# Wider transfers of queries, outputs and cached keys in attention, top-k in two mixed groups, gates split at 10, and an order planned with longer issue times

## The chip, the cores and the metric

The kernel runs on one core of one Trainium2 chip, as one launch. The metric is the time of a run on the device in microseconds (us); lower is better. A core has TensorE (matmuls; PE in the profile, PEld for its weight loads), VectorE (DVE), ScalarE (ACT), GpSimd (POOL) and SyncE (SP), which here issues nearly all transfers between memory (HBM) and the chip's buffers. The engines run beside each other, each through its own list of instructions, strictly in order, and wait for each other by semaphores.

## The reference

One layer of a hybrid encoder, for 1024 new positions of one stream (the prompt) and 32 positions of another (the sample), which has 512 positions of cached keys and values. The weights are shared, all data is float32.

```python
h = rmsnorm(x, g_mix)                          # 1024 + 32 rows of 1024
q_a, k_a, v_a, q_i, k_i, w_i, q_b, k_b, v_b, gate_a, gate_b = split(h @ w_in)
# mixer A: 8 heads of 64, q and k normed and rotated
score = sum over 8 index heads of relu(q_i . k_i) * w_i      # the indexer
keep the 256 best keys per row (136 in the sample), of blocks of 64 that are not later
o_a = softmax(q_a . k_a / 8 over the kept keys) @ v_a
# mixer B: 8 heads of 64, stick-breaking attention, strictly causal
o_b = (sigmoid(z) * product over the later keys of (1 - sigmoid(z))) @ v_b
m = sigmoid(gate_a) * (o_a @ w_branch_a) + sigmoid(gate_b) * (o_b @ w_branch_b)
h = x + m @ w_out
y = h + relu(rmsnorm(h) @ w_up)**2 @ w_down     # 1024 -> 4096 -> 1024
```

The outputs are y of both streams and the new keys and values.

## The kernel before

**Matmuls in three passes.** TensorE multiplies in a shortened float32 (`F32R`). To keep the precision every operand is split into a high part and the rest, and a product is made of three matmuls, high x high, high x rest and rest x high (`three`, line 438). A weight comes in units of 128 x 512: `unit` (line 406) loads one into `wst` (3 buffers), ACT casts it to `wh`, POOL subtracts to `wl` (`split`, line 401; 5 buffers each). `column_block` (line 445) runs the matmuls of one output block over its column chunks.

**Stages** (`Layer.run`, line 464). First come normalisation and the index projections, the projections of mixer B (`project_b`), the index scores, top-k, the projections of mixer A (`project_a`) and gates 0 to 5. Each projection stores queries, keys and values, already split, in device memory (`dq`, `dk`, `dv`). Then comes attention in two rounds. The early round takes the first 512 positions: for mixer B, then for A, for each of 8 heads `attend(h, is_a, (0, 2))` (line 1072), and behind heads 2 and 5 `attend_new` (line 1132), which does the sample for four heads at once. Columns of gates 6 to 15 stand beside it as filler. Then `branch` (line 1225) multiplies the outputs with the branch weights, `out` with `w_out`, and `ffn_group` (line 1274) runs up and down projections of the first 512 positions. The late round of attention, for positions 512 to 1023, is a generator, `late`, that is advanced beside this work, EARLY steps before the branch of mixer A and one step for every PACE units in the FFN. At last the second group, the other 512 positions and the sample, goes through `load_o`, `branch`, `out` and the FFN.

**Order by a planner.** The program is not issued as written. `Plan.record` (line 260) notes every instruction with its dependencies and a cost from `cost` (line 203); `Plan.run` (line 332) simulates the five engines with these costs, and always issues, on the engine that is free first, the ready instruction of the best rank, then the earliest in the program. Ranks are FAST, PREP (loads and splits of weights), MAIN, FILL (the matmuls of `column_block`) and SLOW (top-k). So filler matmuls fall where the planner sees a gap. The order on each engine is fixed by this; on the chip an instruction that is late by the plan's times holds everything behind it on its engine. An issue on SP costs 450 ns in the plan, whatever its shape. `Plan.close` (line 134) first issues everything that touches the buffers to be closed; what is recorded later comes behind it on every engine.

**Attention.** For a head, `attend` loads keys `kk` and values `v` (rings of 2), and for each of two tiles of 256 queries two halves of `q` (high and rest, 64 rows each; ring of 3, [128, 2, 256]). Score matmuls go into banks `s`; `softmax_weights` or `stick_weights` makes the weights; TensorE transposes them into banks `t`, `split_pt` splits them, and the product with `v` goes into `po`. `finish` (line 1053) adds the two halves of `po` into an output `o` [64, 256] and stores it in `do`. `attend_new` loads, per head, the cached keys twice (into both halves of the rows, buffer `k32` in the ring of `q`), the new keys, the cached values and the new values, one transfer each.

**Top-k** (`top_k_begin`, line 778, and `top_k`, line 846). The threshold of every row is found bit by bit, 31 bits. In each bit a candidate (`cand`) is tried: count the scores on one side of it, compare the count with the wanted one (`hit`, in a bank called `small`) and keep the candidate where it hits. Tiles of 128 rows have 128 (t + 1) scores a row; tile 8 is the sample with 32 rows of 544. Three groups run beside each other: `v` with tiles 2, 3 and 4, counted on DVE by a comparison with a sum, and `a` (6, 7) and `b` (5, 8), counted on ACT by Sign with a sum. `top_k` then makes the masks; for groups counted on ACT it first finds the lowest kept score (`low`).

**Gates.** `gate(e)` (line 1184) makes 128 gate columns of all 1056 positions in three chunks (`parts`: 512, 272, 272), with two weight units. For e from 6 to 15 the first chunk is done in one call and the other two in a second call, which loads and splits the two units again; SPLIT = 14 says how many of the second calls stand ahead of the branch of mixer B.

Of the kernel before, what the change touches and what calls it, by code (L numbers as in the profile page):

```python
# [27 lines left out]
H = 8  # L28
# [15 lines left out]
SPLIT = 14  # L44
EARLY, PACE = 16, 4
# [43 lines left out]
class Plan:  # L89
# [113 lines left out]
    def cost(self, eng, op, out, ins, scalar, kw):  # L203
# [45 lines left out]
        return 450.0, 450.0  # L249
# [140 lines left out]
class Layer:  # L390
# [73 lines left out]
    def run(self):  # L464
# [94 lines left out]
        self.pr = g1.pool  # L559
        for is_a in (False, True):  # L560
# [16 lines left out]
        late = (None for is_a in (False, True) for h in range(H) for _ in self.attend(h, is_a, (4, 6)))  # L577
# [14 lines left out]
        for j in (1, 0):  # L592
            self.load_o(g2, j)
            self.branch(g2, j)
# [183 lines left out]
    def top_k_begin(self):  # L778
# [12 lines left out]
        class Group:  # L791
# [3 lines left out]
            def __init__(g, name, tiles, act, place):  # L795
# [6 lines left out]
                g.zero = nc.tile(tp, [128, n], F32, f"zero{name}")  # L802
                nc.vector.memset(g.thr, 0)
                nc.vector.memset(g.allb, -1)
                nc.vector.memset(g.zero, 0.0)
                for j, t in enumerate(tiles):
                    m, L, k = size(t)
                    nc.vector.memset(g.want[:, j:j + 1], float(L + 1 - 2 * k if act else k))

            def count(g, at, op, act):  # L810
                cnt = nc.tile(tp, [128, g.n], F32, "cnt", tag="cnt" + g.name, bufs=2)
                for j, t in enumerate(g.tiles):
                    m, L, _ = size(t)
                    if m < 128:
                        nc.vector.memset(cnt[:, j:j + 1], 0.0)
                    junk = nc.tile(tp, [128, 1024], BF16, "junk", tag="junk" + g.name, bufs=1)
                    if act:
# [9 lines left out]
            def step(g, at, hit_op, new):  # L827
                cnt = g.count(at, ALU.is_ge, g.act)
# [3 lines left out]
            def bit(g, b):  # L832
                cand = nc.tile(tp, [128, g.n], I32, "cand", tag="cand" + g.name, bufs=2)
                nc.vector.tensor_scalar(cand, g.thr, 1 << b, None, op0=ALU.bitwise_xor)
                g.step(cand.bitcast(F32), ALU.is_le if g.act else ALU.is_ge, cand)
# [3 lines left out]
        for gs in (self.groups,):  # L839
            for g in gs:  # L840
                g.step(g.zero, ALU.is_gt if g.act else ALU.is_lt, g.allb)
            for b in range(30, -1, -1):
                for g in gs:
                    g.bit(b)

    def top_k(self):

        nc, tp, tx, size = self.nc, self.top, self.top, self.size
        for g in self.groups:
# [3 lines left out]
            if g.act:  # L853
                low = nc.tile(tp, [128, g.n], F32, "low" + g.name)
                for j, t in enumerate(g.tiles):
                    m, L, k = size(t)
                    pen = nc.tile(tx, [128, 1024], F32, "pen", tag="pre", bufs=1)
# [6 lines left out]
            above = g.count(tf, ALU.is_gt, False)  # L864
# [188 lines left out]
    def finish(self, po, dst, n=256):  # L1053

        nc, at = self.nc, self.at
        tmp = nc.tile(at, [64, 256], F32, "ov", bufs=1)
        o = nc.tile(at, [64, 256], F32, "o", bufs=2)
        nc.scalar.copy(tmp, po[64:128])
        nc.vector.tensor_add(o, po[0:64], tmp)
        if n < 256:  # L1060
            s = o.rearrange("e (j i t) -> e j i t", i=2, t=DEC)
            o = nc.tile(at, [64, 256], F32, "on", tag="o", bufs=2)
            nc.vector.tensor_add(o[:, :n].rearrange("e (j t) -> e j t", t=DEC), s[:, :, 0], s[:, :, 1])
        with nc.rank(FAST):
            nc.sync.dma_start(dst, o[:, :n])
# [6 lines left out]
    def attend(self, h, is_a, tiles):  # L1072
# [30 lines left out]

        for t0 in tiles[::-1]:
            yield
            c = 128 * t0
            q = nc.tile(at, [128, 2, 256], F32R, "q", bufs=3)
            for s in range(2):
                nc.sync.dma_start(
                    q.bitcast(F32)[HD * s:HD * s + HD], self.dq[g].rearrange("s e t -> e s t")[:, :, c:c + 256])  # L1110
# [19 lines left out]
            self.finish(po, self.do[g, :, c:c + 256])  # L1130

    def attend_new(self, u, is_a):
# [7 lines left out]
        for i in range(2):  # L1140
            src = self.dq[g0:g0 + 4, i, :, new].rearrange("j e t -> e j t")
            for s in range(2):
                nc.sync.dma_start(qz[64 * s:64 * s + 64, i], src)
        for j in range(4):
            k32 = nc.tile(at, [128, PAST], F32, "k32", tag="q", bufs=3)
            for i in range(2):
                nc.sync.dma_start(k32[HD * i:HD * i + HD], a["ck" + sfx][4 * u + j])
            k = nc.tile(at, [128, SEQ], F32R, "kc", tag="k", bufs=2)[:, :LS]
            nc.sync.dma_start(k.bitcast(F32)[:, :DEC], self.dk[g0 + j].rearrange("s e t -> (s e) t")[:, new])
            nc.scalar.copy(k[:, DEC:], k32)  # L1150
            nc.gpsimd.tensor_sub(k[HD:, DEC:], k32[HD:], k.bitcast(F32)[HD:, DEC:])
            for i in range(2):
                q, first, last = self.qz[:, i, 128 * j:128 * j + 128], j + i == 0, j + i == 4
                nc.tensor.matmul(ps0, q, k[:, DEC:], start=first, stop=last)
                nc.tensor.matmul(ps1[:, :DEC], q, k[:, :DEC], start=first, stop=is_a and last)
# [14 lines left out]
        for j in range(4):  # L1170
            vcs = nc.tile(at, [128, 8, 128], F32R, "vcs", tag="v", bufs=2)[:, 0:4]
            vc = nc.tile(at, [128, 4, HD], F32, "vc", tag="o", bufs=2)
            nc.sync.dma_start(vc, a["cv" + sfx][4 * u + j])
            self.split(vcs[:, :, 0:HD], vcs[:, :, HD:], vc)
# [232 lines left out]
```

## Time and profile before

| | |
|---|---|
| time, 3 runs | 1838.2 us median, 1836.76 to 1841.13 |
| the profiled execution's own time | 1837.8 us |
| its span, first to last instruction | 1836.0 us |
| PE busy | 1792.9 us, 11622 matmuls |
| POOL, DVE, ACT busy | 1017.0, 1054.0, 900.0 us |
| loads of queries (`q<-dq`) | 128 of 128 KB |
| stores of outputs (`do<-o`) | 64 of 64 KB |
| gate weight units (`wst<-w_g`) | 52 of 256 KB |

In the profile a row of busy time by stage gives from and to in us, the length, then busy time of PE, PEld, DVE, ACT and POOL (with the number of instructions), then the granted clock of TensorE as a share of full speed, the busy share of the DMA engines and GB/s. Rows of instructions are named out<-in by the program's buffers; all carry line 381, the planner's issuing line, so one goes by buffers. A wait reads: who waited <- for whom: us in total, times, longest. The chain is the list of work and waits that ended last, followed back from the end. SPq is SP's queue of issues.

### The profile page before, as it was taken

To read this page: it belongs to the slowest core of one execution; us is meant where nothing else is said; L and a number is where in the kernel's file an instruction comes from. 1 tells how busy PE (TensorE), PEld (TensorE's weight loads), DVE (VectorE), ACT (ScalarE), POOL (GpSimd) and SP (SyncE) were. 2 spreads that over 40 slices of the span, in tenths; PEclk is the share of its full clock that TensorE was granted. 3 is DMA by queue.
4 is the path that set the end of the run, shared out by engine and by line. 5 is a ranking of instruction groups with operands and counts; after the bars stand their busy time and mean duration, and the time that the engine had idled before them with its cause. 6 is when DMAs were issued, how large, how long until landed. Compare 5 with 4: busy or idle time off the path is not lost.

```text
span 1836.0 us, 33063 instructions
## 1 busy us (share of the span) xinstructions
PE 1792.9 (98%) x11622; PEld 1649.0 (90%) x11622; DVE 1054.0 (57%) x2323; ACT 900.0 (49%) x1854; POOL 1017.0 (55%) x897
## 2 busy tenths in 40 slices
PE   8999999999999999999999999999999999999999
PEld 7899999999978889878888888888799999999999
DVE  7569998688244565678875555533326633333333
ACT  7356778952145676867755444442225422222221
POOL 4722232335256755698885545565558655555553
PEclk9999999999998999999999999999999999999999
DMA  7134443445566777664343343343365333233323
GB/s 256 55 88 130 130 135 103 130 133 149 167 191 179 220 196 221 194 180 148 99 132 110 114 134 117 107 132 96 92 193 160 101 91 93 87 87 93 87 87 95
DMA packets 170101, 243.85 MB, mean 133 GB/s; under 512 B 29904, under 2 KB 80432, under 8 KB 169936
## 3 DMA queue, kind: packets, MB, share of 16 engines
q1 hardware_dynamic: 169504, 241.41, 44.2%
q8 instruction: 92, 1.51, 0.3%
q14 instruction: 73, 0.60, 0.1%
q10 hardware_dynamic: 432, 0.34, 0.1%
HBM read 189.39 MB, written 52.17 MB: 132 GB/s over the span
## 4 chain that ended last, share of the span: by engine, by line
PE 83%; DVE 7%; DMA 3%; issue 2%; POOL 2%; SPq 1%; ACT 1%; ACTq 0%; DVEq 0%; POOLq 0%
PE pj L381 63%; PE s L381 12%; PE t L381 4%; PE o L381 4%; DVE junk L381 2%; POOL pb L381 1%; SPq L381 1%; DMA q<-dq 1%; DVE small L381 1%; DVE xl L381 1%; DVE pre L381 1%; DMA k<-dk 0%; POOL wl L381 0%; POOL p L381 0%; DMA xt<-x 0%
## 5 line engine op out<-in xcount | busy, mean ns | idle before, releaser
L381 POOL TENSOR_TENSOR wl<-wst,wh 128x512 fp32r<-128x512 f32 x424 | 571.5, 1351 | 482.7 <-ACT wh L381 441.4
L381 PE MATMUL pj<-xh,wh 128*128 128x272 f32 (+2 forms) x2048 | 691.4, 338 | 2.1 <-ACT wh L381 0.8
L381 PE MATMUL pj<-xl,wh 128*128 128x272 f32 (+2 forms) x2048 | 692.2, 338 | 0.1
L381 PE MATMUL pj<-xh,wl 128*128 128x272 f32 (+2 forms) x2048 | 689.9, 338 | 1.0 <-POOL wl L381 0.9
L381 ACT CAST wh<-wst 128x512 fp32r<-128x512 f32 x424 | 262.1, 620 | 485.0 <-PE pj L381 392.2
L381 PEld LDWEIGHTS pj<-xh,wh 128*128 128x128 f32 x2048 | 386.9, 189 | 35.3 <-ACT wh L381 1.5
L381 PEld LDWEIGHTS pj<-xh,wl 128*128 128x128 f32 x2048 | 386.8, 189 | 31.1 <-POOL wl L381 1.5
L381 PEld LDWEIGHTS pj<-xl,wh 128*128 128x128 f32 x2048 | 386.7, 189 | 30.8 <-DVE xl L381 0.3
L381 DVE TENSOR_TENSOR y<-pj,y 128x272 f32<-128x272 f32 (+1 forms) x192 | 100.4, 524 | 196.5 <-PE pj L381 196.0
L381 PE MATMUL pj<-gh,wl 128*128 128x272 f32 x640 | 184.4, 289 | 0.0
L381 PE MATMUL pj<-gl,wh 128*128 128x272 f32 x640 | 184.2, 289 | 0.2 <-POOL gl L381 0.2
L381 PE MATMUL pj<-gh,wh 128*128 128x272 f32 x640 | 182.5, 288 | 0.0
L381 DVE TENSOR_TENSOR xl<-ru,xh 128x272 fp32r<-128x272 f32 (+1 forms) x96 | 107.3, 1119 | 95.4 <-ACT xh L381 95.2
L381 DVE TENSOR_TENSOR tt<-t,tt 128x512 fp32r<-128x512 f32 (+2 forms) x168 | 101.1, 622 | 56.4 <-ACT tt L381 54.9
L381 ACT ACTIVATE junk<-score,cand 128x768 bf16<-128x768 f32 (+3 forms) x124 | 119.2, 961 | 23.2 <-DVE cand L381 22.6
L381 DVE TENSOR_TENSOR_SCAN rem<-rem 128x896 f32<-128x896 f32 (+6 forms) x66 | 112.6, 1727 | 25.5 <-ACT rem L381 25.2
L381 ACT CAST tt<-t 128x512 fp32r<-128x512 f32 (+2 forms) x168 | 85.7, 539 | 75.1 <-PE t L381 54.9
L381 PEld LDWEIGHTS pj<-gl,wh 128*128 128x128 f32 x640 | 120.5, 188 | 0.7 <-POOL gl L381 0.6
L381 PEld LDWEIGHTS pj<-gh,wl 128*128 128x128 f32 x640 | 120.3, 188 | 0.0
L381 PEld LDWEIGHTS pj<-gh,wh 128*128 128x128 f32 x640 | 119.8, 188 | 0.3
L381 PE MATMUL s<-k,q 128*128 128x512 f32 (+3 forms) x384 | 102.6, 365 | 10.1 <-DMA q<-dq 8.4
L381 POOL TENSOR_TENSOR p<-p,rem 128x895 f32<-128x895 f32 (+6 forms) x66 | 102.6, 1566 | 14.3 <-DVE rem L381 11.3
(211 smaller groups left out, 2880.8 us busy)
## 6 DMA issues: line engine op xcount, KB each, us to landing
wst<-w_up SPq DMA_DIRECT2D x128, 256.0 KB, 2.7
wst<-w_down SPq DMA_DIRECT2D x128, 256.0 KB, 2.6
q<-dq SPq DMA_DIRECT2D x128, 128.0 KB, 3.1
wst<-w_g SPq DMA_DIRECT2D x52, 256.0 KB, 3.4
k<-dk SPq DMA_DIRECT2D x48, 256.0 KB, 3.2
v<-dv SPq DMA_DIRECT2D x48, 256.0 KB, 3.7
dv<-vs SPq DMA_DIRECT2D x32, 256.0 KB, 2.3
wst<-w_out SPq DMA_DIRECT2D x32, 256.0 KB, 2.8
```

Source lines behind the costliest of these rows:

```text
L381: fn(*args, **kw)
```

## The change

- Queries: `attend` loads the 512 columns of a head's two tiles at once, two transfers instead of four, into a ring of 2 buffers [128, 2, 512]. The first late head uses the place of `qz`.
- Outputs: both tiles of a head go into one `o` [64, 512] and one store; `halves` takes the place of `finish`.
- The sample: `k32` holds the cached keys of two heads in 64 rows, one transfer for a pair instead of four; the new keys of four heads come in one transfer (`kn`), the new values too (`vn`, now in the ring of the keys), cached values in pairs.
- Top-k: two groups, `a` with tiles 2, 3, 4 and 7 and `b` with 5, 6 and 8; tile 7 of `a` and tiles 5 and 6 of `b` are counted on ACT, the others on DVE. DVE counts "less than" now, so that both counts compare alike.
- Gates 6 to 9 do all chunks in one call; 10 to 15 keep the second call, which stands behind the branch of mixer B (SPLIT 14 to 10).
- Late attention: one step is advanced behind the last head but one of the early round (AHEAD), EARLY goes from 16 to 14.
- The plan: an issue on SP costs 470 ns, and 620 ns for up to 64 rows.
- Second group: both `load_o` stand ahead of the branches, with 4 buffers of their own. FFN: the row factors go into `acc` in place of a tile `rb2` of their own, and two down projections (KEEP) of the last quarter but one move behind the last up projection.

```diff
-SPLIT = 14
-EARLY, PACE = 16, 4
+SPLIT = 10
+AHEAD = 1
+KEEP = (6, 7)
+TOPK = (("a", [2, 3, 4, 7], (7,), 0), ("b", [5, 6, 8], (5, 6), 16))
+EARLY, PACE = 14, 4
...
-        return 450.0, 450.0
+        d = 470.0 if out.shape[0] > 64 else 620.0
+        return d, d
...
+                for _ in range(AHEAD if is_a and h == H - 2 else 0):
+                    next(late)
...
         for e in range(6, 16):
-            self.gate(e, "pb", 3, self.parts[:1])
-        for e in range(6, SPLIT):
-            self.gate(e, "pb", 3, self.parts[1:])
+            self.gate(e, "pb", 3, self.parts if e < SPLIT else self.parts[:1])
...
         for j in (1, 0):
-            self.load_o(g2, j)
+            self.load_o(g2, j, "o32", 4)
+        for j in (1, 0):
             self.branch(g2, j)
...
-            def count(g, at, op, act):
-                cnt = nc.tile(tp, [128, g.n], F32, "cnt", tag="cnt" + g.name, bufs=2)
+            def count(g, at, op, act=()):
+                g.cnts = g.cnts[::-1]
+                cnt = g.cnts[0]
...
-                    if act:
+                    if t in act:
                         nc.scalar.activation(
...
-        self.groups = [Group("v", [2, 3, 4], False, 0), Group("a", [6, 7], True, 16), Group("b", [5, 8], True, 32)]
+        self.groups = [Group(*x) for x in TOPK]
...
+    def halves(self, po, o):
+
+        nc = self.nc
+        nc.scalar.copy(o, po[64:128])
+        nc.vector.tensor_add(o, po[0:64], o)
...
+        c = 128 * tiles[0]
+        if late and g == H:
+            qq = nc.tile(at, [128, 2, 512], F32R, "q", tag="qz")
+        else:
+            qq = nc.tile(at, [128, 2, 512], F32R, "q", bufs=2)
+        for s in range(2):
+            nc.sync.dma_start(
+                qq.bitcast(F32)[HD * s:HD * s + HD], self.dq[g].rearrange("s e t -> e s t")[:, :, c:c + 512])
+        o = nc.tile(at, [64, 512], F32, "o", bufs=2)
         for t0 in tiles[::-1]:
             yield
-            c = 128 * t0
-            q = nc.tile(at, [128, 2, 256], F32R, "q", bufs=3)
-            for s in range(2):
-                nc.sync.dma_start(
-                    q.bitcast(F32)[HD * s:HD * s + HD], self.dq[g].rearrange("s e t -> e s t")[:, :, c:c + 256])
...
+        kn = nc.tile(at, [128, 4, DEC], F32R, "kn", bufs=1)
+        nc.sync.dma_start(kn.bitcast(F32), self.dk[g0:g0 + 4, :, :, new].rearrange("j s e t -> (s e) j t"))
         for j in range(4):
-            k32 = nc.tile(at, [128, PAST], F32, "k32", tag="q", bufs=3)
-            for i in range(2):
-                nc.sync.dma_start(k32[HD * i:HD * i + HD], a["ck" + sfx][4 * u + j])
...
+            if j % 2 == 0:
+                k32 = nc.tile(at, [64, 2, PAST], F32, "k32", tag="q", bufs=2)
+                nc.sync.dma_start(k32, a["ck" + sfx][4 * u + j:4 * u + j + 2].rearrange("j e t -> e j t"))
...
+        vn = nc.tile(at, [128, SEQ], F32R, "vn", tag="k", bufs=2)[:DEC, :512].rearrange("t (j e) -> t j e", j=4)
+        nc.sync.dma_start(vn.bitcast(F32), self.dv[g0:g0 + 4, :DEC, NEW].rearrange("j t e -> t j e"))
...
-        rb2 = nc.tile(g.pool, [128, g.w], F32, f"rb2{i}")
+        rb2 = g.acc
...
+            if q == nq - 1:
+                for e in KEEP:
+                    go_down(e, q - 1)
             for e in range(KB):
-                go_down(e, q)
+                if q != nq - 2 or e not in KEEP:
+                    go_down(e, q)
                 beside(1)
```

More of the change, by code (lines that the diff above doesn't have):

```diff
@@ L559, in run @@
         self.pr = g1.pool
+        late = (None for is_a in (False, True) for h in range(H) for _ in self.attend(h, is_a, (4, 6)))
         for is_a in (False, True):
@@ L802, in __init__ @@
                 g.zero = nc.tile(tp, [128, n], F32, f"zero{name}")
+                g.cnts = [nc.tile(tp, [128, n], F32, f"cnt{name}{i}") for i in range(2)]
+                for c in g.cnts:
+                    nc.vector.memset(c, 0.0)
                 nc.vector.memset(g.thr, 0)
@@ L827, in step @@
             def step(g, at, hit_op, new):
-                cnt = g.count(at, ALU.is_ge, g.act)
+                cnt = g.count(at, ALU.is_lt, g.act)
                 nc.vector.tensor_tensor(g.hit, cnt, g.want, op=hit_op)
@@ L834, in bit @@
                 nc.vector.tensor_scalar(cand, g.thr, 1 << b, None, op0=ALU.bitwise_xor)
-                g.step(cand.bitcast(F32), ALU.is_le if g.act else ALU.is_ge, cand)
-        self.groups = [Group("v", [2, 3, 4], False, 0), Group("a", [6, 7], True, 16), Group("b", [5, 8], True, 32)]
+                g.step(cand.bitcast(F32), ALU.is_le, cand)
+        self.groups = [Group(*x) for x in TOPK]
         self.size = size
[L839 to L844, printed above, removed]
+        for g in self.groups:
+            g.step(g.zero, ALU.is_gt, g.allb)
+        for b in range(30, -1, -1):
+            for g in self.groups:
+                g.bit(b)
     def top_k(self):
@@ L863, in top_k @@
                 tf = low
-            above = g.count(tf, ALU.is_gt, False)
+            above = g.count(tf, ALU.is_gt)
             need = nc.tile(tp, [128, g.n], F32, "need" + g.name)
@@ L1129, in attend @@
                             start=j + i == 0, stop=j + i == t0 + 2)
-            self.finish(po, self.do[g, :, c:c + 256])
+            self.halves(po, o[:, c:c + 256])
+        with nc.rank(FAST):
+            nc.sync.dma_start(self.do[g, :, 128 * tiles[0]:128 * tiles[0] + 512], o)
     def attend_new(self, u, is_a):
@@ L1180, in attend_new @@
                                  start=k == 0, stop=False)
-            nc.tensor.matmul(out, vn[:DEC], now[:DEC, :, 32 * j:32 * j + 32], start=False, stop=True)
-        self.finish(po, self.do[g0:g0 + 4, :, new].rearrange("g e t -> e g t"), 128)
+            nc.tensor.matmul(out, vn[:, j], now[:DEC, :, 32 * j:32 * j + 32], start=False, stop=True)
+        o = nc.tile(at, [64, 512], F32, "o", bufs=2)
+        self.halves(po, o[:, :256])
+        s = o[:, :256].rearrange("e (j i t) -> e j i t", i=2, t=DEC)
+        on = o[:, 256:384].rearrange("e (j t) -> e j t", t=DEC)
+        nc.vector.tensor_add(on, s[:, :, 0], s[:, :, 1])
+        with nc.rank(FAST):
+            nc.sync.dma_start(self.do[g0:g0 + 4, :, new].rearrange("g e t -> e g t"), on)
     def gate(self, e, tag="gz", bufs=2, parts=None):
@@ L1289, in done @@
                 r = g.tmp("ru", "pb", 3)
[L1290 removed]
+                nc.vector.scalar_tensor_tensor(r, ps, 0.0, rb2[c], op0=ALU.max, op1=ALU.mult)
                 nc.gpsimd.tensor_mul(r, r, r)
```

51 lines of the change are left out of this document (19 added, 32 removed).

## The prediction

> **What bounds the kernel now.** I read the page first, then busy time by stage, then who TensorE waited for in the worst stage, then the DMA queue's own instructions there.
>
> ```profile
> span 1836.0 us, 33063 instructions
> ...
> PE 1792.9 (98%) x11622; PEld 1649.0 (90%) x11622; DVE 1054.0 (57%) x2323; ACT 900.0 (49%) x1854; POOL 1017.0 (55%) x897
> ```
>
> TensorE is the bound. The profiled execution took 1837.8 us: the span of 1836.0 and 1.8 around it; the median of the runs, 1838.2, lies 0.4 above it. The change leaves TensorE's matmuls as they are, so it can only win back what is not work: 1836.0 - 1792.9 = 43.1 us of idle time, and time at a lower clock. The stages, with busy time of PE, PEld, DVE, ACT and POOL, then the granted clock:
>
> ```profile
> 0.00:200.00 200.00, 188.29 (x1196) 175.70 (x1197) 150.19 (x388) 114.28 (x261) 87.33 (x109) 0.99 0.43 129
> 200.00:300.00 100.00, 94.95 (x595) 93.41 (x595) 88.70 (x360) 77.46 (x165) 30.96 (x30) 0.98 0.46 139
> 300.00:460.00 160.00, 154.64 (x1187) 149.74 (x1186) 131.19 (x357) 95.06 (x216) 69.50 (x71) 1.00 0.43 129
> 460.00:520.00 60.00, 60.00 (x365) 53.83 (x365) 14.40 (x33) 9.92 (x20) 12.85 (x11) 1.00 0.49 148
> 520.00:760.00 240.00, 227.61 (x1426) 203.50 (x1425) 128.98 (x299) 157.00 (x340) 160.51 (x155) 0.97 0.71 208
> 760.00:900.00 140.00, 135.63 (x767) 115.56 (x767) 111.36 (x111) 100.31 (x206) 117.67 (x66) 0.99 0.53 158
> 900.00:1420.00 520.00, 519.18 (x2817) 445.03 (x2816) 265.42 (x494) 230.46 (x431) 315.70 (x250) 1.00 0.41 124
> 573.00:580.00 7.00, 5.05 (x28) 3.87 (x27) 6.51 (x8) 4.17 (x11) 5.28 (x6) 0.97 0.64 178
> 580.00:590.00 10.00, 10.00 (x37) 8.83 (x36) 2.23 (x3) 3.76 (x9) 3.09 (x4) 0.51 0.53 161
> 685.00:689.00 4.00, 4.00 (x21) 4.00 (x20) 1.95 (x13) 1.32 (x3) 2.12 (x3) 0.57 0.84 257
> ```
>
> TensorE's idle time is length minus PE: 11.7 us in the first 200 (mostly the start, which the change does not reach), 5.1 in 200 to 300 and 5.4 in 300 to 460 (top-k, on a full DVE), none in 460 to 520 (gates alone), 12.4 in 520 to 760 (the early attention), 4.4 in 760 to 900, 0.8 in 900 to 1420. The last three rows show a second price: behind an idle stretch of 573 to 580 (1.95 us) the clock is about half for 10 us.
>
> What ends the idle time of 520 to 760 are two kinds of load, 9.8 us in all:
>
> ```profile
> PE s L381 <- DMA q<-dq: 8.4, 6, 2.9
> PE s L381 <- DMA kc<-dk: 1.4, 2, 0.8
> ```
>
> The longest, 2.9 us, is at 681. SP's own instructions just before it, and the chain there:
>
> ```profile
> 678.84 0.55 SPq L381 DMA_DIRECT2D dg<-gz  x1
> 679.45 1.24 SPq L381 DMA_DIRECT2D qz<-dq  x2
> 680.79 1.22 SPq L381 DMA_DIRECT2D q<-dq  x2
> ```
>
> ```profile
> 681.40 2.74 DMA q<-dq
> ```
>
> Each issue starts within 0.2 us of the end of the one before: SP is doing nothing but issuing, and the query load stands last in that line. TensorE waits not for bandwidth but for the queue's turn. The planner books 450 ns for every issue (`cost`, line 203), and here each takes 0.55 to 0.62; so its order is one that SP can't keep.
>
> **Part A, the wider transfers.** Prices of an issue on SP (min/median/max ns, then first and last start):
>
> ```profile
> L381 SPq DMA_DIRECT2D q<-dq x68: 573/586/681, 521.4 to 742.9; - x68
> ...
> L381 SPq DMA_DIRECT2D do<-o x64: 451/482/1604, 541.5 to 1210.0; - x64
> ...
> L381 SPq DMA_DIRECT2D k<-ckb x16: 471/510/596, 535.1 to 601.7; - x16
> ...
> L381 SPq DMA_DIRECT2D kc<-dk x16: 326/456/1237, 536.3 to 709.3; - x16
> ```
>
> In the early attention 16 heads load queries four times each (two tiles, two halves); now twice: 32 fewer, 32 x 0.586 = 18.8 us of SP. Outputs, one per head instead of two: 16 x 0.482 = 7.7. The sample's cached keys were loaded twice per head, 32 in all (half of them the row's `ckb`); now once per pair of heads, 8: 24 x 0.51 = 12.2. Its new keys go from 16 issues to 4, 12 x 0.456 = 5.5, and its new values too, which I price at the least of the keys' row, 12 x 0.326 = 3.9. Together 48 us, a fifth of the stage's 240, are taken off a queue that is overloaded in stretches. I expect the gapless lines to break up, the more so as the new order books 620 ns for transfers of up to 64 rows. One wait is new in kind: a wide query load that finds its slot taken holds SP, and behind it stand the weight loads of the filler; the plan orders by that slot too, so I price it at nothing here and in the second rival at its bound. ACT's and POOL's work on the keys keeps its length: as many columns on fewer rows.
>
> The gain: the 9.8 us of waits; and the clock behind them, (1 - 0.51) x 10 = 4.9 at 580 and (1 - 0.57) x 4 = 1.7 at 685: 16.4. I take 15, for a wide load lands later for the first of its two tiles. Bounds: 0 (next waits take its place), and 12.4 + 0.03 x 240 = 19.6, all idle time and all slow clock of the stage.
>
> Is the clock to be counted? The row at 580 says yes, behind a stretch of 7 us with 1.95 us idle in pieces. The Trainium skill (TensorE: Matmul & The Clock Gate, section "Why this matters for your kernels") asks for no idle gap of over about 3 us, since a whole window of idleness brings the half clock back; by it the stretch at 580 has another cause, and the gain would be 11.5 instead of 16.4. The trace disagrees with it here, since no gap in 573 to 580 can be over 1.95 us.
>
> **Part B, the gates split at 10, one late step fewer.** For gates 10 to 13 the last 544 columns move from before `branch(g1, 1)` to behind it, and stay TensorE filler; for 6 to 9 all columns are now done in one pass, so 8 weight units are neither loaded nor split a second time. A unit costs POOL:
>
> ```profile
> L381 POOL TENSOR_TENSOR wl<-wst,wh 128x512 fp32r<-128x512 f32 x424 | 571.5, 1351 | 482.7 <-ACT wh L381 441.4
> ```
>
> 8 x 1.351 = 10.8 us of POOL go, and as many casts on ACT and loads. POOL is the fullest helper of 760 to 900 (117.67 of 140). There late attention starts 15 steps in instead of 16 (1 + 14), and the moved gates bring TensorE work with little POOL work. The idle 4.4 us and 0.01 x 140 = 1.4 of clock are the bound; I take half, 3. Below nothing it could go only if the moved gates came late; the branch before them needs the same outputs as ever.
>
> **Part C, top-k in two mixed groups.**
>
> ```profile
> L381 ACT ACTIVATE junk<-score,cand x124: 727/983/1162, 186.5 to 384.2; 128x768 bf16<-128x768 f32 x31, 32x544 bf16<-32x544 f32 x31, 128x896 bf16<-128x896 f32 x31, 128x1024 bf16<-128x1024 f32 x31
> L381 ACT ACTIVATION_READ_ACCUMULATOR junk<-score,cand x124: 185/186/201, 187.3 to 384.9; 128x1 f32 x93, 32x1 f32 x31
> L381 DVE TENSOR_SCALAR_CACHE_REDUCE junk<-score,cand x93: 602/745/881, 143.3 to 285.2; 128x384 bf16<-128x384 f32 x31, 128x512 bf16<-128x512 f32 x31, 128x640 bf16<-128x640 f32 x31
> L381 DVE DVE_READ_ACCUMULATOR junk<-score,cand x93: 72/82/86, 143.9 to 286.0; 128x1 f32 x93
> ...
> L381 ACT ACTIVATE junk<-score,zeroa x2: 1028/1086/1145, 196.3 to 197.8; 128x896 bf16<-128x896 f32 x1, 128x1024 bf16<-128x1024 f32 x1
> ```
>
> ```profile
> L381 DVE TENSOR_TENSOR small<-cnt,small x96: 143/165/167, 142.2 to 386.6; 128x2 int32<-128x2 f32 x64, 128x3 int32<-128x3 f32 x32
> L381 DVE TENSOR_SCALAR cand<-small x93: 128/159/163, 142.6 to 380.9; 128x2 int32<-128x2 int32 x62, 128x3 int32<-128x3 int32 x31
> L381 DVE COPY_PREDICATED small<-small,cand x93: 146/168/170, 150.7 to 389.4; 128x2 int32<-128x2 int32 x62, 128x3 int32<-128x3 int32 x31
> ```
>
> ```profile
> L381 POOL TENSOR_SCALAR mask<-pre x7: 636/832/1045, 303.0 to 445.6; 128x384 bf16<-128x384 f32 x1, 128x512 bf16<-128x512 f32 x1, 128x640 bf16<-128x640 f32 x1, 128x896 bf16<-128x896 f32 x1
> ```
>
> DVE now spends per bit 3 x (0.745 + 0.082) + 3 x (0.165 + 0.159 + 0.168) = 3.96 us. The change drops one group's small operations (-0.49) and adds the sample's count of 544 columns, about 0.78 between the 512 and 640 columns of the row, plus 0.08: 4.33, or 31 x 0.37 = 11 us more. ACT loses its shortest count: 31 x (0.727 + 0.186) = 28 us less. But the DVE group of tiles 2, 3 and 4 ran alone from 143, a bit in (285.2 - 143.3)/31 = 4.6 us; tied to tile 7 it starts when tile 7 can be counted, which was at 196 (`zeroa`). So 53/4.6 = 11.5 bits of about 3 us of DVE work, at most 34 us, move back, and 11 come on top, 45 in all, into stretches where DVE has 11.3 (200 to 300), 28.8 (300 to 460) and 45.6 us (460 to 520) free. It fits, and the end moves back. A group's `hit` now waits on DVE for ACT's count as well, with the projections' evacuations queued behind it; the two old ACT groups had that wait too. The chain ends at 445.6 in the trace and must end before TensorE's last filler:
>
> ```profile
> 513.93 1.78 DMA dg<-gz
> ```
>
> That leaves 68 us of cover. I expect the chain to end at 470 to 500, hidden, and to cost TensorE 1 us net where DVE is fuller. Bounds: -12 (idle 5.1 + 5.4 and 0.02 x 100 of clock all gone) to +28 (third rival).
>
> **Part D, the rest.** `load_o` ahead of both branches, KEEP and `acc` in place of `rb2` touch 900 to the end, where at most 0.8 us is idle up to 1420: 0.5 gained.
>
> Sum: -15 - 3 + 1 - 0.5 = -17.5; 1837.8 - 17.5 = 1820.3, **1820 us**.
>
> **The rivals.** *More.* Idle time and slow clock of 200 to 1420 all go: 19.6 + 5.8 + 12.5 + 0.8 = 38.7, so 1799. For it: everything is planned anew with truer times. Against it: 300 to 460 has idle time without SP's doing.
>
> *The stall changes its name.* The new values of the sample (`vn`) now sit in the two-slot ring of the keys, so the second head behind each of the 4 sample parts can load keys only after that part's last matmul. With a landing like the 2.74 us above and one issue, 3.4 us, and 1.7 of clock once: 4 x 3.4 + 1.7 = 15.3, which eats part A: 1820.3 + 15.3 = 1836, no change. The same comes out if the queries wait for their ring (two wide slots for three narrow ones) and not for SP: then the change does not do what it says. Against both: SP's gapless line at 681, and eight tiles in flight against six.
>
> *Top-k outlasts the filler (slower).* One place: the closing of the top-k buffers, behind which every attention instruction stands in the plan. The DVE group of before took 4.6 us a bit where it needed about 3. If the two mixed groups, on a DVE that the projections of 300 to 460 fill to 82%, run at half of DVE, 8.7 us a bit, the bits last to 196 + 31 x 8.7 = 466. The masks then take 389.4 to 445.6 as now, 56, and those of the early group, now done in between (303.0 - 285.2), some 18 more: 540. TensorE is dry from 514: 26 us and 1.7 of clock make 1820.3 + 27.7 = 1848. From an end at about 531 on it eats the whole gain.
>
> **How the numbers follow.** A measurement of this kernel can tell about 0.2%, 3.7 us, from no change. The forecast (by itself 1806, with A and B at their upper bounds and C at half of -12, to 1833, with half of A, no B and C at 3) has 0.62, *more* 0.10, the renamed stall 0.12, the long top-k 0.16. Faster 0.72, same 0.12, slower 0.16. The range, 1802 to 1844, takes in the forecast, the renamed stall and part of the two outer cases.
>
> **What would show it.** Right: waits of TensorE for `q` and `kc` in the early attention under 3 us, clock there 0.99 or more, half the query issues at twice the size, the last `mask<-pre` before 514, PE idle under 32 us in all. Wrong: waits of the same stage for `k<-dk` or for helpers in their place; an idle stretch between the last gate and the first score matmul; DVE groups of top-k that run past 460.

## The result and the profile after

| | before | after |
|---|---|---|
| median | 1837.48 us (6 runs, 1836.24 to 1841.13) | 1818.92 us (6 runs, 1816.52 to 1823.79) |
| the profiled execution's own time | 1837.8 us | 1819.17 us |

After takes 0.99 of the time of before, with a 95% interval of 0.9884 to 0.9916: 1.0% faster, some 18 us. The page of after, with the span, the engines' busy time and the row of query loads (KB each, median us from issue to landing):

```profile
span 1817.4 us, 32617 instructions
...
PE 1782.6 (98%) x11622; PEld 1645.4 (91%) x11622; DVE 1059.0 (58%) x2260; ACT 868.0 (48%) x1776; POOL 1013.3 (56%) x889
...
q<-dq SPq DMA_DIRECT2D x64, 256.0 KB, 5.5
```

TensorE runs the same 11622 matmuls. Its idle time is 1817.4 - 1782.6 = 34.8 us instead of 43.1, and its busy time is 10.3 us less for the same matmuls, part of it time at a lower clock. Busy time by stage of after, in the columns of the prediction's rows:

```profile
0.00:200.00 200.00, 187.39 (x1189) 174.77 (x1190) 136.65 (x318) 111.07 (x251) 87.94 (x109) 0.99 0.42 127
200.00:300.00 100.00, 98.96 (x643) 97.99 (x641) 94.49 (x337) 87.46 (x172) 30.85 (x30) 1.00 0.51 156
300.00:460.00 160.00, 155.95 (x1183) 150.94 (x1184) 151.12 (x396) 70.39 (x158) 74.95 (x73) 1.00 0.43 128
...
520.00:760.00 240.00, 229.62 (x1468) 207.04 (x1468) 139.34 (x312) 152.27 (x345) 155.94 (x151) 0.99 0.72 197
760.00:900.00 140.00, 137.62 (x754) 117.07 (x753) 116.22 (x111) 98.59 (x200) 131.12 (x70) 0.99 0.50 143
```

Length minus the first figure is idle time; I count the clock as busy time x (1 - clock), to which the two digits leave about 1 us of play. From 200 to 460 the idle time went from 10.4 to 5.1 us and the clock of 200 to 300 from 0.98 to 1.00: about 7 us won where the prediction had 1 us lost. From 520 to 760 idle time went from 12.4 to 10.4 and the clock from 0.97 to 0.99: 2.0 + 4.5 = 6.5 us, not the 15 of part A. From 760 to 900 it is 2.0 us. The first 200 us lost 0.9. These stages make 15 of the 18.6 us between the two profiled executions. Behind 900, where part D works, TensorE is idle for 4.4 us instead of 4.2, so no gain of it shows; the rest of the 18.6 is busy time that the two digits of the clock can't place.

Who TensorE waited for in 520 to 760, in after:

```profile
PE s L385 <- DMA k<-dk: 4.6, 2, 2.9
PE o L385 <- DVE tt L385: 3.1, 1, 3.1
PE s L385 <- DMA q<-dq: 1.3, 1, 1.3
```

The waits for queries fell from 8.4 to 1.3, as forecast, but waits for keys and for a helper stand in their place, which the prediction had named as a sign of being wrong. The longest wait for a load is at 665. Below are SP's instructions, then TensorE's, then the chain there, then busy time around it (clock, DMA share and GB/s at the end of a row):

```profile
659.50 0.55 SPq L385 DMA_DIRECT2D wst<-w_g  x1
660.14 0.48 SPq L385 DMA_DIRECT2D do<-o  x1
661.05 0.70 SPq L385 DMA_DIRECT2D k<-dk  x1
```

```profile
665.47 0.40 PE L385 MATMUL pj<-xl,wh 128*128 128x512 f32 x1
668.76 0.66 PE L385 MATMUL s<-k,q 128*128 128x384 f32 x1 [2.89 <-DMA k<-dk]
```

```profile
661.05 7.57 DMA k<-dk
```

```profile
660.00:664.00 4.00, 4.00 (x19) 3.25 (x18) 1.15 (x5) 1.52 (x4) 1.88 (x2) 1.00 1.09 265
664.00:668.00 4.00, 1.87 (x9) 1.16 (x7) 0.69 (x1) 2.54 (x4) 0.14 (x2) 1.00 1.04 265
668.00:672.00 4.00, 3.24 (x12) 2.94 (x13) 0.87 (x3) 1.74 (x5) 2.59 (x3) 0.59 0.74 179
```

The keys leave at 661.05 and land only 7.57 us later, while all 16 DMA engines are full (share over 1). Before the wait TensorE has its filler; the next instruction in its fixed order is the score matmul, so it stands for 2.89 us, and behind that the clock is 0.59 for 4 us. At the wait of before at 681 SP issued without a gap; here it is idle from 660.62 (660.14 + 0.48) to 661.05, just ahead of this issue.

Top-k of after, rows of counts and of masks (min/median/max ns, first to last start):

```profile
L385 DVE TENSOR_SCALAR_CACHE_REDUCE junk<-score,cand x124: 601/752/882, 193.2 to 355.2; 128x384 bf16<-128x384 f32 x31, 128x512 bf16<-128x512 f32 x31, 128x640 bf16<-128x640 f32 x31, 32x544 bf16<-32x544 f32 x31
```

```profile
L385 POOL TENSOR_SCALAR mask<-pre x7: 513/833/1258, 374.3 to 438.6; 128x384 bf16<-128x384 f32 x1, 128x512 bf16<-128x512 f32 x1, 128x640 bf16<-128x640 f32 x1, 128x1024 bf16<-128x1024 f32 x1
```

The bits run from 193.2 to 355.2 on DVE, (355.2 - 193.2)/31 = 5.2 us each (the last count on ACT starts at 356.9), and the last mask starts at 438.6, earlier than the 445.6 of before and not at 470 to 500.

### The profile page after: what moved, and what is told of

It reads as the page before. It is cut to its first block, busy times and chain, and to the rows that moved or that the text cites. A ratio compares the mean times of both kernels' runs of the same rounds, so it can differ in the third digit from the quotient of the medians.

```text
span 1817.4 us, 32617 instructions
## 1 busy us (share of the span) xinstructions
PE 1782.6 (98%) x11622; PEld 1645.4 (91%) x11622; DVE 1059.0 (58%) x2260; ACT 868.0 (48%) x1776; POOL 1013.3 (56%) x889
## 4 chain that ended last, share of the span: by engine, by line
PE 88%; DVE 6%; DMA 3%; issue 1%; ACT 1%; POOL 0%; SPq 0%; ACTq 0%; DVEq 0%; POOLq 0%
PE pj L385 65%; PE s L385 13%; PE t L385 5%; PE o L385 4%; DVE junk L385 2%; DMA k<-dk 1%; SPq L385 0%; DMA q<-dq 0%; DVE rw L385 0%; DVE small L385 0%; DVE xl L385 0%; DVE rem L385 0%; DMA do<-o 0%; DMA x<-xT 0%; DMA xt<-x 0%
## 5 line engine op out<-in xcount | busy, mean ns | idle before, releaser
L385 POOL TENSOR_TENSOR wl<-wst,wh 128x512 fp32r<-128x512 f32 x416 | 564.7, 1360 | 470.1 <-ACT wh L385 446.1
L385 ACT CAST wh<-wst 128x512 fp32r<-128x512 f32 x416 | 258.0, 621 | 500.9 <-PE pj L385 390.0
L385 DVE TENSOR_TENSOR xl<-ru,xh 128x272 fp32r<-128x272 f32 (+1 forms) x96 | 99.6, 1038 | 82.9 <-ACT xh L385 82.7
L385 DVE TENSOR_TENSOR_SCAN rem<-rem 128x896 f32<-128x896 f32 (+6 forms) x66 | 117.5, 1800 | 11.9 <-ACT rem L385 10.7
L385 PE MATMUL o<-tt,v 128*128 128x256 f32 (+1 forms) x640 | 107.3, 281 | 5.8 <-DVE tt L385 4.1
L385 PEld LDWEIGHTS o<-tt,v 128*128 128x128 f32 x640 | 96.4, 190 | 17.6 <-DVE tt L385 4.9
```

The costliest lines, as they stand in the source:

```text
L385: fn(*args, **kw)
```

## The experiments

Two theories stood at the start. *Transfers*: the gain comes from fewer and wider transfers, as part A says, or they at least contribute it. *Costs*: it comes from the plan's truer price of an issue, and the wide transfers add little. Later a third was needed, *order*: every edit makes the planner write another order, and that order decides. Ratios are against before, with 95% intervals; 0.001 is 1.8 us.

### One part alone

**x_transfers** takes only the wide queries and outputs, the sample's loads with `vn` in the ring of the keys, and `acc` for `rb2`:

```diff
-            q = nc.tile(at, [128, 2, 256], F32R, "q", bufs=3)
+            qq = nc.tile(at, [128, 2, 512], F32R, "q", bufs=2)
...
+            self.halves(po, o[:, c:c + 256])
+        nc.sync.dma_start(self.do[g, :, 128 * tiles[0]:128 * tiles[0] + 512], o)
...
```

> The kernel before with the wide transfers alone (queries, outputs, the sample's keys and values; and the row factors in `acc`, which makes the room); top-k, gates and the plan's costs stay old. If the transfers carry the gain, as forecast, it takes 1837.5 down by 10 us or more, to 1828 or less. If only a third of it comes from the early attention, as the stages of the changed kernel say (idle and slow clock there fell by some 7 us), it takes 4 to 8 us off. If the old 450 ns for an issue is what makes the order late, wide transfers alone gain under 3 us.

Measured: 1847.79 us, ratio 1.0053 (1.0039 to 1.0067). Alone they make the kernel slower by 10 us. Early attention in two stretches, all instructions and then those of the tile `pj` alone, which are the filler. Before:

```profile
520.00:740.00 220.00, 208.57 (x1302) 186.23 (x1301) 118.83 (x284) 139.54 (x309) 141.60 (x138) 0.97 0.71 209
740.00:800.00 60.00, 55.75 (x350) 48.97 (x349) 42.16 (x50) 47.36 (x97) 47.49 (x34) 0.98 0.63 186
```

```profile
520.00:740.00 220.00, 141.16 (x672) 104.29 (x670) 17.24 (x31) 0.97 0.71 209
740.00:800.00 60.00, 35.45 (x175) 27.48 (x176) 5.64 (x10) 0.98 0.63 186
```

The same two views of x_transfers:

```profile
520.00:740.00 220.00, 215.64 (x1393) 195.40 (x1391) 113.11 (x259) 138.19 (x302) 147.25 (x141) 0.99 0.74 202
740.00:800.00 60.00, 45.89 (x220) 38.85 (x219) 34.66 (x66) 40.29 (x88) 32.00 (x26) 0.77 0.55 154
```

```profile
520.00:740.00 220.00, 158.08 (x800) 121.38 (x798) 20.66 (x37) 0.99 0.74 202
740.00:800.00 60.00, 12.27 (x41) 7.51 (x39) 1.82 (x3) 0.77 0.55 154
```

The profiled execution of x_transfers took 1853.8 us, 6 us over the median of its runs, so the sizes below are those of a long one. Up to 740 part A does what it promised: idle time falls from 11.4 to 4.4 us and the clock rises from 0.97 to 0.99, together 7.0 + 4.1 = 11 us. Then it is given back, and more: from 740 to 800 TensorE is idle for 14.1 us instead of 4.3, at a clock of 0.77 instead of 0.98, together 9.9 + 9.4 = 19 us. The second pair says why. The plan used 800 filler matmuls by 740 instead of 672, so only 41 were left for the end of the early attention, where before had 175; the two together are 841 and 847, nearly the same stock. From 755.2 to 789.9 there is no filler matmul at all: these are the last `pj` matmul ahead of that stretch and the first behind it, from TensorE's timeline:

```profile
755.22 0.63 PE L384 MATMUL pj<-xh,wl 128*128 128x512 f32 x1
...
789.88 1.20 PE L384 MATMUL pj<-xh,wh 128*128 128x512 f32 x2
```

What TensorE waits for most from 740 to 800 are the helpers that make the attention weights:

```profile
PE o L384 <- DVE tt L384: 5.7, 2, 3.3
PE t L384 <- POOL p L384: 3.2, 3, 1.8
PE s L384 <- ACT rem L384: 1.9, 2, 1.7
```

**x_costs** changes one line:

```diff
-        return 450.0, 450.0
+        d = 470.0 if out.shape[0] > 64 else 620.0
+        return d, d
```

> The kernel before with the plan's issue costs of 470 and 620 ns alone. If an order that SP can keep is what mattered, it gains 5 us or more by itself, since the waits for queries get planned around. If the queue is simply too full, the truer cost alone gains under 3 us: PE's wait for queries stays over 5 us. A plan made anew moves the time by a few us in any case.

Measured: 1832.90 us, 0.9967 (0.9954 to 0.998), 6 us faster with no transfer changed. Its early attention, and TensorE's longest waits for loads there:

```profile
520.00:760.00 240.00, 231.90 (x1486) 207.87 (x1485) 133.24 (x305) 159.70 (x348) 168.13 (x158) 0.99 0.75 213
```

```profile
PE s L382 <- DMA q<-dq: 4.1, 5, 1.7
```

Idle time of 520 to 760 falls from 12.4 to 8.1 us and the clock rises from 0.97 to 0.99: 4.3 + 4.5 = 9 us, more than the whole change wins in this stage, and the waits for queries are halved with as many issues on SP as before. About 1 us of it is lost again from 760 to 900, where idle time is 6.7 us instead of 4.4, at a clock of 1.00 instead of 0.99.

**x_topk** takes only the two mixed groups:

```diff
-        self.groups = [Group("v", [2, 3, 4], False, 0), Group("a", [6, 7], True, 16), Group("b", [5, 8], True, 32)]
+        self.groups = [Group(*x) for x in TOPK]
```

> The kernel before with the two mixed top-k groups alone. By the forecast it costs 1 us (1838.5). By the stages of the changed kernel, where 200 to 460 lost 7 us less (idle 10.4 to 5.1, clock 0.98 to 1.00), it gains 5 to 8 us: 1830 to 1832.

Measured: 1836.97 us, 0.9992 (0.9982 to 1.0003): not told from no change. Its profiled execution was the longest of its twelve, 1843.36 us; in it idle time from 200 to 460 falls from 10.4 to 6.7 us, and from 520 to 760 it rises from 12.4 to 16.2.

**x_gates** takes only the split and the late steps:

```diff
-SPLIT = 14
-EARLY, PACE = 16, 4
+SPLIT = 10
+AHEAD = 1
+EARLY, PACE = 14, 4
```

> The kernel before with the gates split at 10, one late step ahead and EARLY 14 alone. By the forecast it gains 3 us (1834.5), by relief of POOL in 760 to 900. If the eight weight units spared matter for the loads of the early attention as well, 5 us or more. If it is nothing but a shift of filler, 0 to 1.

Measured: 1834.05 us, 0.9978 (0.9968 to 0.9988), 4 us faster. Two of its stages:

```profile
520.00:760.00 240.00, 227.72 (x1457) 203.00 (x1456) 130.57 (x307) 156.49 (x345) 154.83 (x149) 0.99 0.71 204
760.00:900.00 140.00, 135.40 (x765) 115.80 (x764) 118.34 (x108) 96.20 (x196) 120.48 (x66) 0.99 0.51 153
```

From 760 to 900, where part B placed its gain, idle time is 4.6 us instead of 4.4 and POOL is a little fuller, 120.48 us for 117.67. The gain stands before that: from 520 to 760 the clock is 0.99 instead of 0.97, some 4.5 us.

The four alone add up to 1.0053 + 0.9967 + 0.9992 + 0.9978 - 3 = 0.9990, 2 us, where the whole change brings 18: the parts don't add. What part D brings besides `acc` was not run by itself.

### The whole change without one part

**y_oldtransfers** is after with the narrow transfers of before, the sample's loads one a head and `finish` among them:

```diff
-            qq = nc.tile(at, [128, 2, 512], F32R, "q", bufs=2)
+            q = nc.tile(at, [128, 2, 256], F32R, "q", bufs=3)
...
```

> The changed kernel with the old narrow transfers of queries, outputs and the sample's data; all else new. If the transfers carry the gain it loses 10 us or more (1829 or over). If they are worth the 7 us that the early attention shows, it stands at 1824 to 1828. If the truer issue costs do their work, under 3 us are lost.

Measured: 1812.25 us, 0.9867 (0.9853 to 0.988). This is faster than after, whose interval starts at 0.9884, and the fastest kernel of the study. Its early attention and its waits of 520 to 760:

```profile
520.00:740.00 220.00, 213.27 (x1375) 191.29 (x1374) 122.92 (x300) 150.33 (x331) 149.17 (x147) 1.00 0.73 209
740.00:800.00 60.00, 58.60 (x353) 50.68 (x352) 52.28 (x53) 42.39 (x89) 50.64 (x27) 1.00 0.61 177
```

```profile
PE s L385 <- DMA q<-dq: 4.4, 4, 1.4
```

SP issues the narrow transfers again here, and yet no wait for queries is longer than 1.4 us and the clock is 1.00 in both stretches. Here, as in x_costs (longest wait 1.7 us), the narrow transfers are issued without the stall of 2.9 us at 681: another order was enough to remove it, with as many issues of these loads.

**y_oldcosts** is after with the old price:

```diff
-        d = 470.0 if out.shape[0] > 64 else 620.0
-        return d, d
+        return 450.0, 450.0
```

> The changed kernel with the plan's old 450 ns for every issue. If the costs matter, it loses 3 us or more and PE's waits for loads in the early attention grow. If with fewer issues the queue has room whatever the plan books, it stays within 2 us of 1819.

Measured: 1829.16 us, 0.9961 (0.9948 to 0.9974): inside the change the new prices bring 0.9961 - 0.99 = 0.0061, 11 us, the largest difference that undoing one part made. Not by shorter waits for loads, though: from 520 to 760 TensorE waits 3.7 us for queries and 1.8 for keys here, 5.5 against the 5.9 of after, where the theory of costs expected more. What is worse stands behind: 772 filler matmuls are used from 520 to 740 and 95 are left from 740 to 800, a stretch with 7.7 us idle at a clock of 0.91, and from 760 to 900 idle time is 6.3 us instead of 2.4. So the 11 us come with the order that the prices make; that the truth of the prices brings them is not shown.

**y_oldtopk** is after with the three groups of before:

```diff
-        self.groups = [Group(*x) for x in TOPK]
+        self.groups = [Group("v", [2, 3, 4], False, 0), Group("a", [6, 7], True, 16), Group("b", [5, 8], True, 32)]
```

> The changed kernel with the three old top-k groups. By the forecast it gains 1 us. By the stages it loses 5 to 8 us (1824 to 1827), with the idle time back in 200 to 300.

Measured: 1821.92 us, 0.9921 (0.9907 to 0.9935), whose interval overlaps with that of after: 0.9921 - 0.99 = 0.0021 would be 4 us, not told apart from none.

**z_cost2** is a measure of what an order is worth by chance:

```diff
-        d = 470.0 if out.shape[0] > 64 else 620.0
+        d = 490.0 if out.shape[0] > 64 else 640.0
```

> The changed kernel with 490 and 640 ns in the plan instead of 470 and 620: nothing else, only another order. If a part of what the single edits show is the luck of an order made anew, it moves by 2 to 6 us in either direction; if not, it stays within 2 us of 1819.

Measured: 1822.46 us, 0.9915 (0.9899 to 0.993): 20 ns in the plan move the ratio by 0.0015, 3 us, within overlapping intervals. One such draw doesn't bound what an order can be worth; w_landing below moves more.

### Why the wide transfers cost time

The rivals were *key ring* (the new values `vn` in the ring of the keys, the prediction's second rival), *bursts* (the size of the query loads) and the chance of the *order*.

**z_vn** loads the new values of each head into an unused part of `vcs`, so that the ring of the keys is free of them:

```diff
-        vn = nc.tile(at, [128, SEQ], F32R, "vn", tag="k", bufs=2)[:DEC, :512].rearrange("t (j e) -> t j e", j=4)
-        nc.sync.dma_start(vn.bitcast(F32), self.dv[g0:g0 + 4, :DEC, NEW].rearrange("j t e -> t j e"))
...
-            vcs = nc.tile(at, [128, 8, 128], F32R, "vcs", tag="v", bufs=2)[:, 0:4]
+            vw = nc.tile(at, [128, 8, 128], F32R, "vcs", tag="v", bufs=2)
+            vcs, vn = vw[:, 0:4], vw[:DEC, 4]
+            nc.sync.dma_start(vn.bitcast(F32), self.dv[g0 + j, :DEC, NEW])
```

> The kernel after, but the new values of the sample no longer sit in the two-slot ring of the keys: each head's 32 x 128 of them is loaded by a small transfer of its own into an unused part of its buffer of cached values (4 transfers a part instead of 1). Theory 'key ring' (the renamed stall of the prediction): in the kernel after, keys are issued at 661.05 and 714.59 only when a slot of that ring comes free and TensorE waits 4.6 us for them; with the ring to the keys alone those waits go, with the two stretches at half clock behind them (2 x 1.7): 1819 - 8 = 1811, and no wait for k<-dk over 1 us. Theory 'bursts' (transfers of twice the size fill the DMA engines and what is behind them lands late): the waits for keys stay or go to queries, 1819 within 4. Theory 'chance of the order' (any edit makes the planner write another order, worth about 3.5 us either way as with 490/640 ns): 1815 to 1823, and the stall may be anywhere.

Measured: 1818.17 us, 0.9894 (0.988 to 0.9907), the time of after. Its longest wait of 520 to 760, and a later stretch:

```profile
PE s L385 <- DMA k<-dk: 3.6, 1, 3.6
```

```profile
880.00:920.00 40.00, 37.20 (x190) 31.45 (x190) 28.13 (x31) 21.89 (x41) 24.15 (x17) 0.91 0.19 53
```

Two waits for keys became one of 3.6 us, elsewhere, and 2.8 us of idle time with a clock of 0.91 turn up at 880 to 920, where after has 1.1 us and 1.00. The key ring as the one cause falls.

**w_halfloads** keeps the wide buffers and fills each with four transfers of 128 KB:

```diff
-        for s in range(2):
-            nc.sync.dma_start(
-                qq.bitcast(F32)[HD * s:HD * s + HD], self.dq[g].rearrange("s e t -> e s t")[:, :, c:c + 512])
+        for d in (256, 0):
+            for s in range(2):
+                nc.sync.dma_start(
+                    qq.bitcast(F32)[HD * s:HD * s + HD, :, d:d + 256],
+                    self.dq[g].rearrange("s e t -> e s t")[:, :, c + d:c + d + 256])
```

> The kernel after, with the buffers of queries as wide as before this edit, but each filled by four transfers of 128 KB instead of two of 256 KB (32 more issues in the early attention). Theory 'bursts': the narrow loads land in about 3.5 us again instead of 5.1, the keys behind them too, and TensorE's waits in 520 to 760 go: about 1812. Theory 'key ring': nothing changes for the keys, their waits of 4 to 5 us stay and SP has 32 x 0.6 us more to issue: 1819 to 1823. Theory 'chance of the order': 1815 to 1823 with waits of another kind.

Measured: 1815.69 us, 0.9882 (0.9869 to 0.9896), between after and y_oldtransfers and not separated from either. The query loads land earlier, in 3.8 us in the middle instead of 5.0, but the waits for keys in 520 to 760 stay, which is not what *bursts* expected. They, those from 740 to 800 alone, and the two stretches:

```profile
PE s L385 <- DMA k<-dk: 4.0, 3, 2.9
```

```profile
PE s L385 <- DMA k<-dk: 3.6, 2, 2.9
```

```profile
520.00:740.00 220.00, 218.82 (x1421) 197.14 (x1421) 122.27 (x301) 147.98 (x329) 144.50 (x147) 1.00 0.72 206
740.00:800.00 60.00, 55.10 (x280) 46.23 (x278) 45.30 (x45) 39.54 (x81) 51.12 (x27) 0.91 0.51 143
```

Up to 740 only 1.2 us are idle, the least of the kernels shown here, and then 4.9 us and a clock of 0.91 follow. This is not the trade of x_transfers: 128 filler matmuls are left from 740 to 800 (after has 142), and 3.6 of the 4.9 us are waits for keys.

**w_oldsample** is after with the sample loaded as before, its new values in a buffer of their own, queries and outputs wide:

```diff
-                k32 = nc.tile(at, [64, 2, PAST], F32, "k32", tag="q", bufs=2)
-                nc.sync.dma_start(k32, a["ck" + sfx][4 * u + j:4 * u + j + 2].rearrange("j e t -> e j t"))
+            k32 = nc.tile(at, [128, PAST], F32, "k32", tag="q", bufs=2)
+            for i in range(2):
+                nc.sync.dma_start(k32[HD * i:HD * i + HD], a["ck" + sfx][4 * u + j])
...
```

> The kernel after with the sample's part loaded as before (cached keys twice a head, new keys, cached values and new values one transfer a head, the new values in a buffer of their own and not in the ring of the keys), queries and outputs still wide. Theory 'key ring': about 1811 to 1813, like z_vn, though SP issues some 50 transfers more; no long wait for k<-dk. Theory 'bursts': the wide query loads stay, so 1817 to 1821. Theory 'chance of the order': 1815 to 1823.

Measured: 1828.12 us, 0.995 (0.9937 to 0.9964), 9 us slower than after, which none of the three expected. Beside wide queries the sample is better loaded wide, though with everything narrow the kernel is fastest; or else it is the order. The edit is also not quite the sample of before: its new values have one buffer instead of two, and the cached keys a ring of two instead of three. Filler is not what ran out here (151 matmuls from 740 to 800, 4.5 us idle at a clock of 1.00). Of the 6 us between the profiled executions (1825.44 and 1819.17) 3 are idle time from 760 to 900, 5.3 us instead of 2.4; the rest is not placed.

**w_landing** leaves every instruction of after as it is, and only tells the plan that a wide load of up to 64 rows lands 1.6 us later than it booked:

```diff
+        n.more = 1600 if n.size >= 1 << 18 and out.shape[0] <= 64 else 0
...
-            n.end = self.pipe + 1500
+            n.end = self.pipe + 1500 + n.more
```

> The kernel after, but the planner books 1.6 us more until the data of a transfer of 256 KB into at most 64 rows is there (it booked about 3.6 us for a wide query load; in the kernel after they land in 5.1 us in the middle, 8.0 at most). The instructions are the same, only their order can change. Theory 'unknown landing' (the wide loads cost time because the plan sets score matmuls where their queries are not there yet, and what stands behind them on TensorE is held): waits for queries and keys in 520 to 760 fall from 6 us to under 2 and the time comes to 1812 or so, like the narrow transfers. Theory 'chance of the order' (every edit that alters the plan moves the time by some 3 to 4 us, and the five orders so far with wide transfers are draws around 1818): 1814 to 1823, with as much lost in other places. Theory 'key ring': the waits for keys stay, 1818 to 1820.

Measured: 1834.02 us, 0.997 (0.9959 to 0.9981): 0.997 - 0.99 = 0.007, 13 us slower than after, with as many instructions, 32617. All instructions and the filler alone:

```profile
520.00:740.00 220.00, 214.64 (x1374) 193.19 (x1372) 119.31 (x272) 138.82 (x307) 142.40 (x139) 0.99 0.72 194
740.00:800.00 60.00, 49.00 (x234) 39.90 (x234) 46.17 (x65) 43.65 (x92) 41.76 (x27) 0.86 0.53 153
```

```profile
520.00:740.00 220.00, 154.29 (x768) 116.56 (x766) 20.00 (x36) 0.99 0.72 194
740.00:800.00 60.00, 16.67 (x59) 11.36 (x60) 3.98 (x6) 0.86 0.53 153
```

*Unknown landing* falls: waits for queries and keys did shrink, from 4.6 + 1.3 = 5.9 to 2.7 us:

```profile
PE s L386 <- DMA q<-dq: 1.4, 1, 1.4
...
PE s L386 <- DMA k<-dk: 1.3, 2, 0.9
```

Yet the kernel is slower. In the early attention filler is again what ran out: 768 matmuls by 740, and 59 behind it, in a stretch that is idle for 11.0 us at a clock of 0.86. After has 720 and 142:

```profile
520.00:740.00 220.00, 147.46 (x720) 110.22 (x719) 19.66 (x35) 0.98 0.74 201
740.00:800.00 60.00, 36.69 (x142) 24.82 (x143) 5.93 (x9) 0.97 0.53 151
```

## Why the prediction was right, and where it was not

1820 us forecast, 1818.92 measured: the sum was right, and most of its terms were not. That it came out to within about a microsecond is luck. By the stages part A's 15 us came as 6.5, which is 8.5 too little, and part C's loss of 1 came as a gain of 7, which is 8 too much; the two misses cancel.

**Part A failed, in size and as a cause.** The step that failed is the last one, from "9.8 us of waits and the clock behind them" to "I take 15". Of its pieces the issues did go as counted (64 query loads of 256 KB for 128), and waits for queries and cached keys fell to 1.3 us, under the 3 forecast. But the stage won 6.5 us, not 15, and the time doesn't need the transfers: without them the rest of the change takes 1812 us. The reading of 681 was not complete either: SP issued without a gap there, but a queue with fewer issues was not what it took, since x_costs and y_oldtransfers issue the narrow loads as before and have no wait for queries over 1.7 and 1.4 us. What the sum left out is that filler taken early is missing later. I priced idle time of 520 to 760 as if it could be removed by itself; x_transfers removed 11 us of idle time and slow clock up to 740 and paid 19 at the end of the same attention.

**The costs had no term.** I mentioned the 470 and 620 ns only as help for part A. The edit of the prices is worth 6 us alone, and the row of x_costs shows it where part A looked for its gain; inside the change it is 11, more than any other part, but there the waits for loads are not what differs. Both are single orders, and w_landing shows an order to be worth as much.

**Part B was right in size and not in place.** 3 us forecast, 4 measured alone (2 to 6 by the interval). The relief of POOL came, 1008.4 us busy in all of x_gates instead of 1017.0, but not from 760 to 900, and the time was won as clock from 520 to 760. So the size is luck.

**Part C had the wrong sign.** I let the end of the masks move back to 470 to 500 and charged 1 us. The step that failed is adding 45 us of DVE work "into stretches where DVE has" room as if the old end had been set by DVE's work: DVE did get fuller, 94.49 of 100 us in 200 to 300 and 151.12 of 160 in 300 to 460, but the groups that ended last were the two counted on ACT, at (384.2 - 186.5)/31 = 6.4 us a bit by the prediction's row; two mixed groups need 5.2, and their last count on ACT starts 27 us earlier (356.9 against 384.2). The stages of 200 to 460 give 7 us less lost time in after; of it the runs give 1.5 us (alone) and 4 us (inside) to top-k, neither told apart from none.

**Part D** was put at 0.5, and idle time behind 900 shows nothing of it.

**The rivals.** *The stall changes its name* was partly what happened: the waits are for `k<-dk`, and the first is for the keys that are issued at 661.05, behind the last matmuls with the sample's cached keys:

```profile
L385 PE MATMUL s<-kc,qz x8: 388/394/398, 651.9 to 658.7; 128*128 128x512 f32 x8
```

Its price was put at 15.3 us; there are two waits instead of four, 4.6 us in all, with a slow clock behind the first that is worth 0.41 x 3.24 = 1.3 us. Taking `vn` out of the ring did not bring the time back. *Top-k outlasts the filler* did not happen for top-k (the 82% of DVE on which it rested, 131.19 of 160 us, counted top-k's own work in); the same mechanism, filler used up before the work it hides, is what x_transfers and w_landing show one stage later. *More* did not happen. Of the signs named in advance, the clock of the early attention (0.99), the size of the query loads and the last mask came true, as did the waits for `q` and `kc` under 3 us, and PE idle under 32 us did not (34.8).

**Loads of twice the size land later.** Query loads from 520 to 760, in after (time of an issue in ns, then us to landing) and then in before:

```profile
L385 SPq DMA_DIRECT2D q<-dq x34: 579/586/1303, 523.0 to 725.8; - x34
...
DMA to landing us min/median/max: 3.6/5.0/8.0
```

```profile
DMA to landing us min/median/max: 2.7/3.3/5.5
```

The Trainium skill (DMA: Bandwidth & Descriptors, section "Rules for kernel authors") advises to coalesce many small transfers into a large one, and calls transfers under 64 KB mostly overhead. Nothing here speaks for it at 128 KB a query load: cutting the wide load back into four gave 0.9882 against 0.99, no loss for twice the issues, and the halves landed in 3.8 us in the middle. The one run that could speak for it is w_oldsample, 9 us slower with the sample's loads cut smaller, where the order is a rival.

**What stays open.** Why the whole is 0.99 - 0.9867 = 0.0033, 6 us, faster with narrow transfers than with wide ones is not settled. Neither the ring (z_vn) nor the size of the loads (w_halfloads) explains it alone, both together were not tried, and every one of these kernels has an order of its own; w_landing shows that the order alone, with equal instructions, moves the time by 13 us. So the prices of single parts of this change, its truer costs among them, are not known to better than that, and which part brings the 18 us stays open.

## What to carry to other kernels

Where a fixed stock of filler hides a stage, idle time won at its start is worth something only if the filler still lasts to the stage's end: count filler matmuls in its last tenth before and after, not only the waits that go. Where a planner writes the order, time every change of its prices by itself, for a truer one can win 6 us or lose 13, and compare any other edit with what such a change does to the time. And undo each part inside the whole: here the part that carried the forecast took 6 us from the gain, in the one order that was tried.

## What the runs showed that was not expected

- An issue on SP takes as long for a load of 256 KB as for one of 128: `q<-dq` took 586 ns in the middle in both kernels. Its landing took 5.0 us in the middle instead of 3.3.
- With the DMA engines' share at 1.04 to 1.09 a load of keys took 7.57 us from issue to landing.
- A stretch of 2.13 us idle in 4 (664 to 668 in after) was followed by a clock of 0.59 over the next 4 us. A whole stretch that leaned on helpers without filler ran at 0.77 (x_transfers, 740 to 800).
- A truer figure made a plan worse: with the landing of wide query loads nearer to what the profile shows, the kernel lost 13 us.
